# A two-layer hybrid diffusion block: Strassen products reordered, output sums regrouped, block-end splits deferred, modulation weights on GpSimd's queue

## The chip, the cores and the metric

The kernel runs on one core of a Trainium2 chip. The metric is device time in microseconds, the median over runs. Before the change it is 1779.36 us (two runs, 1778.30 and 1780.42).

## What is computed

Two layers over 512 latent and 256 context tokens of width 1024, all in float32. Cut to what matters here:

```python
for layer in range(2):
    mod_x = silu(c) @ ada_w[layer] + ada_b[layer]        # 6144 shifts, scales and gates; mod_c likewise from c_ctx
    hx = modulate(rmsnorm(x, norm1_g), sh1, sc1)         # and hc for the context
    mx, mc = hybrid_mixer(hx, hc, ...)                   # retention and gated linear attention
    x = x + g1 * (mx @ w_out)
    hx = modulate(rmsnorm(x, norm2_g), sh2, sc2)
    x = x + g2 * (square(relu(hx @ w_mlp1)) @ w_mlp2)    # 1024 -> 4096 -> 1024
    # in layer 0 the context goes the same way
return rmsnorm(x, final_g)
```

## The kernel before

Activations lie transposed, features on the 128 partitions and 768 tokens in the row. Each float32 operand is kept as a rounded part "hi" and a rest "lo", and each product is three matmuls: hi by hi, hi by lo, lo by hi (L525 to L527, L1409). Weights come in slabs of 128x1024 (512 KB) through SyncE's DMA queue into a pool of NRAW raw buffers; ScalarE casts hi (L246, L521) and VectorE subtracts for lo (L247, L522). Split slabs stand in a ring of NSPL = 5.

The order on every engine is that in which the program records its instructions. `run` (L467) goes through a list of items; before and after an item `advance` splits slabs up to AHEAD = 4 slabs ahead, as far as ring and raw buffers allow. Chains (ScalarE and VectorE steps that finish a product) are recorded a step at a time, at each tick.

The change acts on the MLP of layer 0. The 32 hidden tiles of 128 features are made in eight blocks of four. From the second block on, two tiles at a time (a "pair" j) are made by Strassen's scheme: seven products of 12 matmuls over 384 columns instead of eight (`strassen_items`, L1427). A `Pair` has four parts: part 0 holds a11 and a12, part 1 s2 and s3, part 2 s1 and a22, part 3 (in a ring of one) s4. The products are recorded as p1, p6, p7, p5, p2, p4, p3. ScalarE copies p1 out (L1450); VectorE adds the others up (L1444: u2, u3, c22, c21, c12). p2 is accumulated onto p1's PSUM bank, p4 onto p7's, p3 onto p5's, so each must follow the read of what the bank held. Of each output quarter, `hidden_chain` makes relu and square on ScalarE (hidh, L1422) and the rest on VectorE (hidl, L1425). After the two pairs of a block, `m2_part` multiplies the block's four hidden tiles by w_mlp2 (matmuls into `pm`) and VectorE adds the result to x (`residual`, L634). The first such item takes four banks and goes over hidden tiles 0 and 1 for all of them before it goes to tiles 2 and 3.

Between these items stand "ada" items. Each calls `ada_sums` (L389) once, which makes layer 1's modulation on VectorE: 64 steps, each with one 128x768 piece of ada_w, multiplied by two columns and added to two sums (L405 for the first of eight, then L407). After eight steps TensorE adds over the partitions (L415), ScalarE copies (L328), TensorE transposes (L333). The pieces come through SyncE's queue into the raw pool.

Of the kernel before, what the change touches and what calls it, by code (L numbers as in the profile page):

```python
# [16 lines left out]
P = 128  # L17
# [13 lines left out]
WCOL = 1024  # L31
NSLOT = 46
NSPL = 5
NRAW = 5
AHEAD = 4
# [3 lines left out]
class Item:  # L39


    def __init__(self, name, fn, slabs=(), deps=(), ahead=AHEAD):
        self.name, self.fn, self.slabs, self.deps, self.ahead = name, fn, list(slabs), list(deps), ahead


# [92 lines left out]
def build(ctx: ExitStack, tc, a):  # L138
# [29 lines left out]
    def chunks(t):  # L168
        return t.rearrange("p (c v) -> p c v", v=P)
# [219 lines left out]
    def ada_sums(l):  # L389
        acc = [work(f"adaacc_{l}_{v}") for v in range(2)]  # L390
        todo = [(u, kk) for u in range(6 * D // T) for kk in range(KK)]

        def load(i):
            u, kk = todo[i]
            w = wraw.tile([P, WCOL], F32, tag="raw", name=f"adaw_{l}_{u}_{kk}")
            nc.sync.dma_start(w[:, 0:T], a["ada_w"][l, kk * P : (kk + 1) * P, u * T : (u + 1) * T])
            return w[:, 0:T]

        nxt = load(0)
        for i, (u, kk) in enumerate(todo):  # L400
            w = nxt
            for v in range(2):
                c = cs[:, kk, v : v + 1]
                if kk == 0:
                    nc.vector.tensor_scalar(acc[v], w, c, None, op0=ALU.mult)  # L405
                else:
                    nc.vector.scalar_tensor_tensor(acc[v], w, c, acc[v], op0=ALU.mult, op1=ALU.add)  # L407
            if i + 1 < len(todo):
                nxt = load(i + 1)
            yield  # L410
            if kk == KK - 1:
                pt = psa.tile([P, 512], F32, tag="psa", name=f"ada_{l}_{u}")
# [54 lines left out]
    def run(plan):  # L467
# [9 lines left out]
        def load_next(must):  # L477

            nonlocal loaded
            if loaded == len(order):  # L480
                return False
            limit = NRAW - (2 if ada_queue else 1) - order[loaded].raws
            if order[loaded].raws and sum(x.held for x in order[:loaded]) > limit:
                assert not must
                return False
            order[loaded].load()
            loaded += 1
            return True
# [21 lines left out]
        for i, it in enumerate(plan):  # L510
            for s in it.slabs:
                need = max(need, order.index(s) + 1)
            advance(i, need + it.ahead)
            assert ready >= need, it.name
            it.fn()
            ch.tick()
            if it.slabs:
                advance(i + 1, need + AHEAD)
# [185 lines left out]
    seg = const.tile([P, T], U8, name="seg")  # L704
    maskb = const.tile([P, NCH, P], U8, name="maskb")
    lgam = const.tile([P, nrd], F32, name="lgam")
# [5 lines left out]
    def setup():  # L712
        nc.vector.memset(seg, 1.0)
        nc.vector.memset(chunks(seg)[:, :, 0:1], 0.0)
        for c in range(NCH):
            nc.vector.tensor_scalar(maskb[:, c], late["delta"], 0.0, None, op0=ALU.is_lt)

# [25 lines left out]
    def layer(l, norm):  # L743
# [29 lines left out]
        def tables(h):  # L773
# [4 lines left out]
            nc.scalar.activation(tmp, late["delta"], AF.Exp, scale=lgneg[:, gb : gb + 1])  # L778
            nc.vector.copy_predicated(d_, maskb[:, 0], tmp)
            nc.scalar.activation(rtab[:, 1], late["ramp"][:, 0], AF.Exp, scale=lgam[:, gf : gf + 1])  # L780
# [116 lines left out]
        def gla(h):  # L897
# [55 lines left out]
            def S():  # L953
# [10 lines left out]
                for (c0, c1), (pf, pb) in zip(CQ, pts):  # L964
                    n = (c1 - c0) * P
                    nc.scalar.copy(am[:, c0 * P : c1 * P], pf[:, 0:n])
                    nc.vector.copy_predicated(
                        am[:, c0 * P : c1 * P], maskb[:, c0:c1].rearrange("p c t -> p (c t)"), pb[:, 0:n]
                    )

# [456 lines left out]
        def strassen_items(j):  # L1427
# [24 lines left out]
            def p6():  # L1452
                product(pair, "s2", "t2", open_(2))
                out(2, "u2", st["p1"])

            def p7():
                product(pair, "s3", "t3", open_(3))
                out(3, "u3", st["u2"])

            def p5():  # L1460
                product(pair, "s1", "t1", open_(4))
                tail(out(4, "c22", st["u3"]), 1, H)

# [5 lines left out]

            def p4():  # L1470
                product(pair, "a22", "t4", p[3], False)
                tail(out(3, "c21", st["u2"]), 1, 0)

            def p3():
                product(pair, "s4", "b22", p[4], False)
                tail(out(4, "c12", st["u2"]), 0, H)

            for i, (fn, x) in enumerate(((p1, 0), (p6, 1), (p7, 1), (p5, 2), (p2, 0), (p4, 2), (p3, 3))):
                plan.append(Item(f"st{i}.{j}", fn, [pair.parts[x]]))
                if i % 2:  # L1480
                    plan.append(Item("ada", mlp_ada))
# [225 lines left out]
```

## Time and profile before

| | |
|---|---|
| median of two runs | 1779.36 us |
| profiled execution | 1778.82 us, span 1777.0 us |
| TensorE matmul busy | 1634.8 us (92%) |
| VectorE busy | 1076.0 us (61%) |
| ScalarE busy | 707.8 us (40%) |
| GpSimd busy | 152.8 us (9%) |
| DMA | 175.56 MB, 99 GB/s on average |

The page gives each engine's share of busy time in 40 slices of some 44 us; below them stands PEclk, the TensorE clock granted, in tenths of full speed. A list of waits names who waited for whom. A timeline row is: start, duration, engine, line, operation, output<-inputs, and in brackets the idle time just before it with its releaser. Matmuls of the same kind overlap, so their rate is read from the distance of their starts.

### The profile page before, as it was taken

The page shows a single profiled execution, that of the slowest core. Times are in us where ns is not written, and L with a number is a line of the kernel's source. Part 1 is how long each engine was busy: PE and PEld are TensorE (multiplying, and loading weights), DVE is VectorE, ACT ScalarE, POOL GpSimd, SP SyncE. Part 2 cuts the span into 40 slices and gives each one's busy share as a digit, 9 for nine tenths or more (in the row PEclk, how much of TensorE's full clock was granted, in tenths as well). Part 3 has the DMA queues.
Part 4 walks back from the last instruction along what each step waited for, and adds up shares of the span by engine and source line. Part 5 has one row for each costly group of instructions (what it writes and reads, how often), then busy time and mean ns, then how long its engine had stood idle before and what let it go on. Part 6 is the DMA issues. An engine that isn't in the chain of part 4 may idle for free.

```text
span 1777.0 us, 22807 instructions
## 1 busy us (share of the span) xinstructions
PE 1634.8 (92%) x9072; PEld 1404.2 (79%) x9072; DVE 1076.0 (61%) x1720; ACT 707.8 (40%) x1223; POOL 152.8 (9%) x159
## 2 busy tenths in 40 slices
PE   5899999999897978698879889999999899999998
PEld 3678888988796868587768777878888888888887
DVE  6575754656776767576667457658756744444445
ACT  5536335644623232332233244645355542222232
POOL 2200022100200000000000002000210210000000
PEclk9999999999998989899989999999999999999999
DMA  9334332221213333333334123122113323333311
GB/s 334 130 124 149 119 114 78 92 77 65 87 31 124 95 109 102 107 107 112 99 104 128 48 89 97 50 63 81 48 52 127 119 86 102 98 96 100 101 59 48
DMA packets 60777, 175.56 MB, mean 99 GB/s; under 512 B 6560, under 2 KB 18400, under 8 KB 60672
## 3 DMA queue, kind: packets, MB, share of 16 engines
q1 hardware_dynamic: 58400, 166.62, 29.2%
q0 software_dynamic: 2272, 7.50, 1.2%
q8 instruction: 71, 1.16, 0.3%
q14 instruction: 34, 0.28, 0.1%
HBM read 169.90 MB, written 4.19 MB: 98 GB/s over the span
## 4 chain that ended last, share of the span: by engine, by line
PE 64%; DVE 17%; ACT 8%; DMA 6%; issue 5%; SPq 0%; POOL 0%; DVEq 0%; ACTq 0%; POOLq 0%
PE pm L526 10%; PE pm L527 10%; PE pm L525 10%; DMA adaw<-in_ada_w 5%; DVE adaacc L407 4%; PE ps_g L527 2%; PE ps_g L525 2%; PE ps_g L526 2%; PE pro L1128 1%; DVE x L634 1%; PE ps_vr L526 1%; PE ps_vr L525 1%; PE ps_vr L527 1%; DVE lo_m L247 1%; PE ps_vg L525 1%
## 5 line engine op out<-in xcount | busy, mean ns | idle before, releaser
L526 PE MATMUL pm<-hidl,hi_m 128*128 128x512 f32 (+1 forms) x800 | 288.5, 361 | 29.6 <-DVE hidl L1425 25.8
L525 PE MATMUL pm<-hidh,hi_m 128*128 128x512 f32 (+1 forms) x800 | 288.5, 361 | 22.8 <-ACT hidh L1422 22.8
L527 PE MATMUL pm<-hidh,lo_m 128*128 128x512 f32 (+1 forms) x800 | 285.9, 357 | 0.0
L526 PEld LDWEIGHTS pm<-hidl,hi_m 128*128 128x128 f32 x800 | 157.6, 197 | 53.3 <-DVE hidl L1425 28.3
L525 PEld LDWEIGHTS pm<-hidh,hi_m 128*128 128x128 f32 x800 | 157.5, 197 | 48.5 <-ACT hidh L1422 24.4
L634 DVE SCALAR_TENSOR_TENSOR x<-pm,mod,x 128x512 f32<-128x512 f32 (+1 forms) x200 | 121.3, 641 | 112.3 <-PE pm L527 112.3
L527 PEld LDWEIGHTS pm<-hidh,lo_m 128*128 128x128 f32 x800 | 157.2, 197 | 20.5
L246 ACT CAST hi_m<-raw_m 128x1024 fp32r<-128x1024 f32 x100 | 104.1, 1041 | 93.2 <-PE pm L526 93.2
L407 DVE SCALAR_TENSOR_TENSOR adaacc<-adaw,cs,adaacc 128x768 f32<-128x768 f32 x112 | 108.8, 1013 | 50.3 <-DMA adaw<-in_ada_w 50.3
L526 PE MATMUL pm<-yl,hi_m 128*128 128x512 f32 (+1 forms) x352 | 128.0, 364 | 2.1 <-DVE yl L620 2.1
L525 PE MATMUL pm<-yh,hi_m 128*128 128x512 f32 (+1 forms) x352 | 128.3, 365 | 0.0
L527 PE MATMUL pm<-yh,lo_m 128*128 128x512 f32 (+1 forms) x352 | 127.7, 363 | 0.5 <-DVE lo_m L247 0.5
L247 DVE TENSOR_TENSOR lo_m<-raw_m,hi_m 128x1024 fp32r<-128x1024 f32 x98 | 120.1, 1226 | 11.5 <-ACT hi_m L246 8.5
L1323 DVE TENSOR_TENSOR hidl<-relu,hidh 128x512 fp32r<-128x512 f32 (+1 forms) x44 | 28.5, 649 | 160.9 <-POOL relu L1321 160.9
L1409 PE MATMUL pst<-yh,hi_m1s 128*128 128x384 f32 x224 | 76.9, 343 | 5.0 <-ACT p L1450 5.0
L526 PEld LDWEIGHTS pm<-yl,hi_m 128*128 128x128 f32 x352 | 67.4, 192 | 13.0 <-DVE yl L620 2.9
L247 DVE TENSOR_TENSOR lo_wi<-raw_wi,hi_wi 128x1024 fp32r<-128x1024 f32 x49 | 59.2, 1224 | 29.1 <-ACT hi_wi L246 29.1
L1409 PE MATMUL pst<-yl,hi_m1s 128*128 128x384 f32 x224 | 76.2, 340 | 0.0
L527 PEld LDWEIGHTS pm<-yh,lo_m 128*128 128x128 f32 x352 | 67.4, 191 | 10.9 <-DVE lo_m L247 1.0
L1409 PE MATMUL pst<-yh,lo_m1s 128*128 128x384 f32 x224 | 75.9, 339 | 0.0
L525 PEld LDWEIGHTS pm<-yh,hi_m 128*128 128x128 f32 x352 | 67.4, 191 | 10.1
L1319 ACT ACTIVATE relu<-pm 128x512 f32<-128x512 f32 (+1 forms) x44 | 23.6, 537 | 128.8 <-PE pm L527 128.8
(358 smaller groups left out, 3877.1 us busy)
## 6 DMA issues: line engine op xcount, KB each, us to landing
raw_m<-in_w_mlp SPq DMA_DIRECT2D x100, 512.0 KB, 3.4
raw_wi<-in_w_in SPq DMA_DIRECT2D x58, 512.0 KB, 3.5
adaw<-in_ada_w SPq DMA_DIRECT2D x64, 384.0 KB, 3.3
adaw<-in_ada_w SPq DMA_DIRECT2D x32, 512.0 KB, 4.7
raw_m1s<-in_w_mlp SPq DMA_DIRECT2D x28, 512.0 KB, 3.9
adaw<-in_ada_w SPq DMA_DIRECT2D x32, 256.0 KB, 6.3
raw_wo<-in_w_out SPq DMA_DIRECT2D x16, 512.0 KB, 3.5
x<-in_xT POOLq DMA_DIRECT2D x8, 384.0 KB, 3.6
```

Source lines behind the costliest of these rows:

```text
L246: nc.scalar.copy(self.hi, self.raw)
L247: self.engine.tensor_sub(self.lo, self.raw, f32(self.hi))
L407: nc.vector.scalar_tensor_tensor(acc[v], w, c, acc[v], op0=ALU.mult, op1=ALU.add)
L525: nc.tensor.matmul(out, wh, xh, start=first, stop=False)
L526: nc.tensor.matmul(out, wh, xl, start=False, stop=False)
L527: nc.tensor.matmul(out, wl, xh, start=False, stop=last)
L634: nc.vector.scalar_tensor_tensor(xs[kk][:, t0:t1], pt[:, 0 : t1 - t0], mod[l][:, v, gate + kk : gate + kk + 1], xs[kk][:, t0:t1], op0=ALU. ...
L1128: nc.tensor.matmul(dst, w, x, start=m == 0, stop=m == len(terms) - 1)
L1319: nc.scalar.activation(r, pt[:, 0 : t1 - t0], AF.Relu)
L1323: nc.vector.tensor_sub(a_.lo[:, t0:t1], r, f32(a_.hi[:, t0:t1]))
L1409: nc.tensor.matmul(pt[:, 0:H], wt[:, w], xt, start=first and k == 0 and i == 0, stop=k == KH - 1 and i == 2, skip_group_check=True,)
```

## The change

Strassen's products are recorded as p1, p6, p5, p7, p3, p4, p2. The sums become u2 = p1+p6, u4 = u2+p5, c22 = u4+p7, c12 = u4+p3, c21 = (p7 bank with p4 added)+u2, c11 = p1 bank with p2 added. p3 has a bank of its own. The last product of each block is marked quiet: no slab is split or loaded after it, and before the item that follows only as many as that item needs. The pieces of ada_w have two tiles of their own (two more slots of 128x768) and come through GpSimd's queue; there is one raw buffer less, and the rule that limits how many slabs are held is fitted to that. `ada_sums` gives up control twice more before L415. The mask of the attention scores is kept once and read through a repeating access pattern instead of six copies.

```diff
-NSLOT = 46
+NSLOT = 48
-NRAW = 5
+NRAW = 4
...
     def ada_sums(l):
         acc = [work(f"adaacc_{l}_{v}") for v in range(2)]
+        ws = [work(f"adaw_{l}_{i}") for i in range(2)]
...
-            w = wraw.tile([P, WCOL], F32, tag="raw", name=f"adaw_{l}_{u}_{kk}")
-            nc.sync.dma_start(w[:, 0:T], a["ada_w"][l, kk * P : (kk + 1) * P, u * T : (u + 1) * T])
-            return w[:, 0:T]
+            nc.gpsimd.dma_start(ws[i % 2], a["ada_w"][l, kk * P : (kk + 1) * P, u * T : (u + 1) * T])
+            return ws[i % 2]
...
             if kk == KK - 1:
+                yield
+                yield
...
-            limit = NRAW - (2 if ada_queue else 1) - order[loaded].raws
+            limit = NRAW - (2 if ada_queue else 0) - order[loaded].raws
...
-            advance(i, need + it.ahead)
+            advance(i, need + (0 if i and plan[i - 1].quiet else it.ahead))
...
-            if it.slabs:
+            if it.slabs and not it.quiet:
                 advance(i + 1, need + AHEAD)
...
-    maskb = const.tile([P, NCH, P], U8, name="maskb")
+    maskb = const.tile([P, P], U8, name="maskb")
...
-                    nc.vector.copy_predicated(
-                        am[:, c0 * P : c1 * P], maskb[:, c0:c1].rearrange("p c t -> p (c t)"), pb[:, 0:n]
-                    )
+                    nc.vector.copy_predicated(chunks(am)[:, c0:c1], rep(maskb, c1 - c0), chunks(pb[:, 0:n]))
...
+            def p5():
+                product(pair, "s1", "t1", open_(3))
+                out(3, "u4", st["u2"])
+
             def p7():
-                product(pair, "s3", "t3", open_(3))
-                out(3, "u3", st["u2"])
-
-            def p5():
-                product(pair, "s1", "t1", open_(4))
-                tail(out(4, "c22", st["u3"]), 1, H)
+                product(pair, "s3", "t3", open_(4))
+                tail(out(4, "c22", st["u4"]), 1, H)
+
+            def p3():
+                product(pair, "s4", "b22", open_(5))
+                tail(out(5, "c12", st["u4"]), 0, H)
+
+            def p4():
+                product(pair, "a22", "t4", p[4], False)
+                tail(out(4, "c21", st["u2"]), 1, 0)
...
-            for i, (fn, x) in enumerate(((p1, 0), (p6, 1), (p7, 1), (p5, 2), (p2, 0), (p4, 2), (p3, 3))):
+            steps = ((p1, 0), (p6, 1), (p5, 2), (p7, 1), (p3, 3), (p4, 2), (p2, 0))
+            for i, (fn, x) in enumerate(steps):
                 plan.append(Item(f"st{i}.{j}", fn, [pair.parts[x]]))
+                plan[-1].quiet = 2 * j % UT == 2 and i == 6
...
-    nc = _bacc.Bacc("TRN2", target_bir_lowering=False, num_devices=1, dynamic_dma_scratch_size=2048)
+    nc = _bacc.Bacc("TRN2", target_bir_lowering=False, num_devices=1, dynamic_dma_scratch_size=1024)
```

VectorE at a block's end (pairs 6 and 7, the fourth block), before. c_0_7 are the output sums of pair 7, hidl_14 and hidl_15 the rests of hidden tiles 2 and 3, lo_m slabs of w_mlp2, everything with m1s_8 belongs to the next pair's weights, x_0 is the first residual after the block's end:

```order
L1444 TENSOR_TENSOR c_0_7_6069<-pst_0_7_5994,u_0_7_5988 128x384
L407 SCALAR_TENSOR_TENSOR adaacc_0_4596<-adaw_3_6_6031,cs,adaacc_0_4596 128x768
L407 SCALAR_TENSOR_TENSOR adaacc_1_4597<-adaw_3_6_6031,cs,adaacc_1_4597 128x768
L1425 TENSOR_TENSOR hidl_15_6025<-c_0_7_6069,hidh_15_6024 128x384
L247 TENSOR_TENSOR lo_m_0_15_6080<-raw_m_0_15_5945,hi_m_0_15_6079 128x1024
L1444 TENSOR_TENSOR c_0_7_6099<-pst_0_7_6009,u_0_7_5988 128x384
L522 TENSOR_TENSOR lo_m1s_8_6105<-raw_m1s_8_0_5971,hi_m1s_8_6104 128x1024
L297 TENSOR_TENSOR s_m1s_8_6108<-raw_m1s_8_0_5971,raw_m1s_8_1_5973 128x512
L298 TENSOR_TENSOR raw_m1s_8_1_5973<-raw_m1s_8_1_5973 128x512
L1425 TENSOR_TENSOR hidl_14_6049<-c_0_7_6099,hidh_14_6048 128x384
L634 SCALAR_TENSOR_TENSOR x_0_3350<-pm_0_3_0_0_6111,mod_147,x_0_3350 128x512
```

The same place now (L406 is the old L405, L637 the old L634, L248 the old L247, L525 the old L522):

```order
L1444 TENSOR_TENSOR c_0_7_6020<-pst_0_7_5951,u_0_7_5934 128x384
L406 TENSOR_SCALAR adaacc_0_4591<-adaw_0_4593,cs 128x768
L406 TENSOR_SCALAR adaacc_1_4592<-adaw_0_4593,cs 128x768
L1425 TENSOR_TENSOR hidl_15_5967<-c_0_7_6020,hidh_15_5966 128x384
L1425 TENSOR_TENSOR hidl_14_6000<-c_0_7_6041,hidh_14_5999 128x384
L637 SCALAR_TENSOR_TENSOR x_0_3345<-pm_0_3_0_0_6046,mod_147,x_0_3345 128x512
L637 SCALAR_TENSOR_TENSOR x_0_3345<-pm_0_3_0_512_6047,mod_147,x_0_3345 128x256
L637 SCALAR_TENSOR_TENSOR x_1_3347<-pm_0_3_1_0_6048,mod_147,x_1_3347 128x512
L637 SCALAR_TENSOR_TENSOR x_1_3347<-pm_0_3_1_512_6049,mod_147,x_1_3347 128x256
L248 TENSOR_TENSOR lo_m_0_14_6103<-raw_m_0_14_5890,hi_m_0_14_6102 128x1024
L248 TENSOR_TENSOR lo_m_0_15_6107<-raw_m_0_15_5892,hi_m_0_15_6106 128x1024
L525 TENSOR_TENSOR lo_m1s_8_6115<-raw_m1s_8_0_5917,hi_m1s_8_6114 128x1024
```

Two lo_m and the first three steps of the next pair's split stand behind the first four residuals instead of among the last sums; hidl_14 is made from c_0_7_6041, which ScalarE takes from PSUM, and no longer from a VectorE sum.

ScalarE between the two pairs of a block (pair 6, then pair 7), before. L1467 is the copy of c11 with relu, hi_m1s_7 with 128x1024 is part 2 of pair 7, with 128x512 part 3, p_0_7 is p1 of pair 7:

```order
L1467 ACTIVATE c_0_6_5889<-pst_0_6_5795 128x384
L1422 ACTIVATE hidh_12_5891<-c_0_6_5889 128x384
L1423 ACTIVATE c_0_6_5889<-c_0_6_5889 128x384
L521 CAST hi_m1s_7_5896<-raw_m1s_7_1_5474 128x1024
L1421 ACTIVATE c_0_6_5912<-c_0_6_5912 128x384
...
L1423 ACTIVATE c_0_6_5934<-c_0_6_5934 128x384
L521 CAST hi_m1s_7_5939<-raw_m1s_7_0_5472 128x512
L246 CAST hi_m_0_12_5947<-raw_m_0_12_5709 128x1024
L1450 COPY p_0_7_5965<-pst_0_7_5951 128x384
```

The same place now (L1475 is c11's copy, L524 the old L521):

```order
L1475 ACTIVATE c_0_6_5877<-pst_0_6_5746 128x384
L1422 ACTIVATE hidh_12_5841<-c_0_6_5877 128x384
L1423 ACTIVATE c_0_6_5877<-c_0_6_5877 128x384
L524 CAST hi_m1s_7_5882<-raw_m1s_7_1_5509 128x1024
L524 CAST hi_m1s_7_5886<-raw_m1s_7_0_5507 128x512
L247 CAST hi_m_0_12_5894<-raw_m_0_12_5673 128x1024
L1450 COPY p_0_7_5911<-pst_0_7_5898 128x384
```

Part 2 of the second pair is split behind all sums of the first pair instead of two sums earlier, since its ring slot holds the first pair's part 0, which p2, now the last product, still reads.

## Rows read from the trace of the kernel before

**Rows 1.** Who waited for whom, TensorE, 515 to 1062 us: total us, times, longest.
```profile
PE pm L526 <- DVE hidl L1425: 25.8, 7, 4.1
PE pm L525 <- ACT hidh L1422: 22.8, 7, 4.7
PE ada L415 <- DVE adaacc L407: 19.5, 12, 6.0
PE pst L1409 <- DVE u L1444: 9.4, 6, 2.9
PE pst L1409 <- ACT p L1450: 5.0, 3, 2.3
PE adat L333 <- ACT adarow L328: 5.0, 4, 2.7
```

**Rows 2.** Windows: span, PE, PEld, DVE, ACT, POOL busy (count), PEclk, DMA share, GB/s.
```profile
515.00:1062.00 547.00, 459.56 (x2482) 412.09 (x2481) 357.89 (x524) 169.01 (x283) 0.00 (x0) 0.93 0.32 99
646.50:734.00 87.50, 70.57 (x374) 63.04 (x374) 59.94 (x85) 24.57 (x41) 0.00 (x0) 0.92 0.35 107
986.00:1058.00 72.00, 63.12 (x348) 58.16 (x348) 37.20 (x56) 24.50 (x41) 0.00 (x0) 0.95 0.18 59
```

**Rows 3.** Timeline, TensorE, the first m2 item behind the fourth block.
```profile
734.05 0.58 PE L525 MATMUL pm<-hidh,hi_m 128*128 128x512 f32 x1 [3.93 <-ACT hidh L1422]
738.60 0.80 PE L526 MATMUL pm<-hidl,hi_m 128*128 128x512 f32 x1 [3.97 <-DVE hidl L1425]
```

**Rows 4.** Timeline, VectorE, the same place.
```profile
728.87 1.95 DVE L407 SCALAR_TENSOR_TENSOR adaacc<-adaw,cs,adaacc 128x768 f32<-128x768 f32 x2 [0.89 <-DMA adaw<-in_ada_w]
730.73 0.55 DVE L1425 TENSOR_TENSOR hidl<-c,hidh 128x384 fp32r<-128x384 f32 x1
...
732.34 0.55 DVE L1444 TENSOR_TENSOR c<-pst,u 128x384 f32<-128x384 f32 x1
735.52 1.22 DVE L522 TENSOR_TENSOR lo_m1s<-raw_m1s,hi_m1s 128x1024 fp32r<-128x1024 f32 x1 [2.63 <-ACT hi_m1s L521]
...
737.99 0.55 DVE L1425 TENSOR_TENSOR hidl<-c,hidh 128x384 fp32r<-128x384 f32 x1
```

**Rows 5.** Timeline, ScalarE, the c11 chain of pair 7 and the cast behind it.
```profile
722.12 0.47 ACT L1467 ACTIVATE c<-pst 128x384 f32<-128x384 f32 x1
...
723.18 0.52 ACT L1423 ACTIVATE c<-c 128x384 f32<-128x384 f32 x1
723.61 1.04 ACT L246 CAST hi_m<-raw_m 128x1024 fp32r<-128x1024 f32 x1
```

**Rows 6.** Groups by line, 515 to 1062 us: busy us, mean ns, idle before.
```profile
L407 DVE SCALAR_TENSOR_TENSOR adaacc<-adaw,cs,adaacc 128x768 f32<-128x768 f32 x112 | 108.8, 1013 | 50.3 <-DMA adaw<-in_ada_w 50.3
L405 DVE TENSOR_SCALAR adaacc<-adaw,cs 128x768 f32<-128x768 f32 x16 | 9.1, 615 | 0.1
```

**Rows 7.** Page, DMA issues: KB each, median us from issue to landing.
```profile
raw_wi<-in_w_in SPq DMA_DIRECT2D x58, 512.0 KB, 3.5
...
x<-in_xT POOLq DMA_DIRECT2D x8, 384.0 KB, 3.6
```

**Rows 8.** Timeline, VectorE: residuals and steps late in a block.
```profile
768.12 1.94 DVE L407 SCALAR_TENSOR_TENSOR adaacc<-adaw,cs,adaacc 128x768 f32<-128x768 f32 x2
771.15 1.14 DVE L634 SCALAR_TENSOR_TENSOR x<-pm,mod,x 128x512 f32<-128x512 f32 x2 [0.49 <-PE pm L527]
776.39 1.94 DVE L407 SCALAR_TENSOR_TENSOR adaacc<-adaw,cs,adaacc 128x768 f32<-128x768 f32 x2
```

**Rows 9.** Timeline, TensorE: Strassen matmuls, starts at full and at half rate.
```profile
631.52 0.33 PE L1409 MATMUL pst<-yl,hi_m1s 128*128 128x384 f32 x1
631.70 0.33 PE L1409 MATMUL pst<-yh,lo_m1s 128*128 128x384 f32 x1
...
632.44 0.52 PE L1409 MATMUL pst<-yh,lo_m1s 128*128 128x384 f32 x1
632.76 0.52 PE L1409 MATMUL pst<-yh,hi_m1s 128*128 128x384 f32 x1
```

More of the change, by code (lines that the diff above doesn't have):

```diff
@@ L43, in __init__ @@
         self.name, self.fn, self.slabs, self.deps, self.ahead = name, fn, list(slabs), list(deps), ahead
+        self.quiet = False
 class Chains:
@@ L714, in setup @@
         nc.vector.memset(chunks(seg)[:, :, 0:1], 0.0)
-        for c in range(NCH):
-            nc.vector.tensor_scalar(maskb[:, c], late["delta"], 0.0, None, op0=ALU.is_lt)
+        nc.vector.tensor_scalar(maskb, late["delta"], 0.0, None, op0=ALU.is_lt)
         re = sp.tile([P, nrd], F32, name="re", bufs=1)
@@ L778, in tables @@
             nc.scalar.activation(tmp, late["delta"], AF.Exp, scale=lgneg[:, gb : gb + 1])
-            nc.vector.copy_predicated(d_, maskb[:, 0], tmp)
+            nc.vector.copy_predicated(d_, maskb, tmp)
             nc.scalar.activation(rtab[:, 1], late["ramp"][:, 0], AF.Exp, scale=lgam[:, gf : gf + 1])
@@ L1468, in p2 @@
                 tail(c, 0, 0, False)
[L1470 to L1476, printed above, removed]
-            for i, (fn, x) in enumerate(((p1, 0), (p6, 1), (p7, 1), (p5, 2), (p2, 0), (p4, 2), (p3, 3))):
+            steps = ((p1, 0), (p6, 1), (p5, 2), (p7, 1), (p3, 3), (p4, 2), (p2, 0))
+            for i, (fn, x) in enumerate(steps):
                 plan.append(Item(f"st{i}.{j}", fn, [pair.parts[x]]))
+                plan[-1].quiet = 2 * j % UT == 2 and i == 6
                 if i % 2:
```

## The prediction, made before the changed kernel ran

> **What bounds the kernel now.** I read the windows first, then TensorE's list of waits, then the timeline at one place. The windows show the one stretch that the change can shorten: from 515 to 1062 us, the MLP of layer 0, TensorE is busy 459.6 of 547 us at a granted clock of 0.93 [rows 2]. The list of waits names its idle time there: 25.8 + 22.8 = 48.6 us behind the hidden tiles (hidl, hidh), 19.5 behind adaacc, 9.4 behind the sum u, 5.0 behind the copy p, 5.0 behind adarow, in all 87.5 us [rows 1]. The first two come seven times, once per block.
>
> Idle time costs twice. Strassen's matmuls start 0.18 us apart at full rate and 0.32 us apart in other places [rows 9]: the two levels, 2.4 and 1.2 GHz. A mean of 0.93 over 547 us means 0.07 x 547 = 38 us lost by the clock, an estimate from that one row. In the last block, where fewer additions for the modulation are left, the clock is 0.95 with 37.2 us of VectorE work instead of 59.9, and still 72.0 us go by [rows 2]. I therefore charge 38 / 87.5 = 0.43 us of clock to each us of idle; the most that could go is 87.5 + 38 = 125 us.
>
> The timeline shows what the seven waits are. TensorE stands 3.93 us for hidh, works off the first half of the item, and stands 3.97 us for hidl [rows 3]. VectorE is the late one: between the last sums it waits 0.89 us for a piece of ada_w, adds 1.95 us of modulation, splits a slab, and only at 732.34 makes the last sum; then, for the next pair, it waits 2.63 us for ScalarE's cast and does three steps before the last hidl at 737.99 [rows 4]. So one engine, in order, has more in these 30 us than it can do.
>
> **The change, part by part.** The sum is against the profiled execution, 1778.8 us, which is 0.6 below the median.
>
> *Block end (48.6 us).* Two lo_m of 1.22 us and the wait of 0.89 us leave VectorE's queue ahead of the last sums: 3.3 of the 3.93 us. Behind the last sum the next pair's split goes: from 732.34 to 737.99 are 5.65 us, of which ScalarE's three steps need 723.18 + 0.52 - 722.12 = 1.6 [rows 5]; the 4.0 saved are the second wait. Since the last product is now p2, its result even skips VectorE's sum. What is deferred, two lo_m of 1.22 and the first split of the next pair, some 5 us, falls behind the first residuals, where the work on four banks covers it; without that cover it costs 5 us a block. I leave 0.6 a block, rounded up to 1: 7 us. Bounds: 0 and 48.6.
>
> *Modulation on GpSimd's queue (19.5 us).* VectorE waits 50.3 us for these pieces [rows 6], since they queue on SyncE behind slabs that wait for a buffer. Now a piece starts when the step before the last one is done. A transfer of the same size on that queue lands 3.6 us after issue [rows 7]; from the end of one step (768.12 + 1.94) to the start of the second next (776.39) are 6.3 us [rows 8], so 2.7 us are left. If VectorE is packed, a step and two residual pairs lie between, 1.94 + 2 x 1.14 = 4.2 us [rows 8], which is still enough. Two more calls stand between a group's last step and the sum over partitions. A call is two products apart, 2 x 12 x 0.18 = 4.3 us, or a tile of m2; two exceed the longest wait, 6.0 us. The 19.5 go; bounds 0 and 19.5. What is late next is the step itself, but nobody waits for it within a group. The 88 calls that are now needed are fewer than the 90 ada items, so nothing of it is left over for layer 1.
>
> First the row that speaks on this queue: of VectorE's operations on those pieces only L405 runs at a quick rate, 615 ns where L407 takes 1013 ns for the same 768 columns, 9.1 us in all [rows 6]. The Trainium skill (SBUF — State Buffer, "SBUF: two separate sides") says against this part of the change that GpSimd cannot write the descriptors of its transfers while VectorE runs an operation that takes both of its ports. By that rule the issues could be held for those 9.1 us at worst, spread over eight groups and within 2.7 us of slack each; the sum would be the same, and the rival on this queue gets a small chance.
>
> *The order of the products (9.4 + 5.0 us).* p's copy is now five products old when p2 needs its bank: 5.0 go, bounds 0 and 5.0. In the place of the wait for u comes one for c22. p4 is accumulated onto p7's bank, with one product (2.2 us) between where there were two (4.3). With VectorE as late as now, the six waits would each grow by 2.2 (13 us), and eight other pairs would wait up to 2.2 (17 us): 9.4 + 13 + 17 = 40 us at most, 0 at least if VectorE is on time. Relieved of its 50.3 us of waiting and of 5 us at each block's end, it is nearer to on time; I take 1 us a pair, 14 us.
>
> *A new wait: part 2 of the second pair.* Its ring slot holds part 0 of the first pair, which p2 reads last; p5, now third, needs it two products and two matmuls later, 4.7 us. In between stand c11's chain and the cast, 722.12 to 724.65, 2.5 us [rows 5], and lo, 1.22 us: 3.8 us. There is 0.9 us of slack if VectorE is on time. Behind the cast in ScalarE's queue wait two more casts and p's copy, for which VectorE's u2 waits. Bounds: 0, and 4 us a block as in the longest hidl wait [rows 1]. VectorE has a modulation step of 1.95 us just ahead; one such step late gives 1, two give 3; I take 2, so 14 us.
>
> *Edits together.* One raw buffer fewer: the slabs of w_in are loaded a slab later. I cost it at nothing, since SyncE runs several slabs ahead of the casts; without that cover a late load costs at most its 3.5 us [rows 7]. The mask through a repeating pattern, the setup's five fewer compares, the two tiles and the smaller descriptor buffer lie beside TensorE's work in the mixer; nothing.
>
> *Sum.* Idle left: 7 + 14 + 14 + 5 (adarow) = 40 of 87.5. Saved: 47.5, and 0.43 x 47.5 = 20.6 by the clock: 68 us. 1778.8 - 68 = **1711 us**.
>
> **The rivals.**
>
> *Nearly all waits go.* If VectorE is on time, c22 and part 2 cost nothing and 5 to 25 us are left. For it: VectorE is busy 59.9 of 87.5 us in a block [rows 2]. Against it: in a block of 70 us that is over 80%, in order, with waits for ScalarE between. At 5 us left: 82.5 x 1.43 = 118, so 1661 us; up to 1689. Chance 0.16.
>
> *VectorE stays late and the waits move inside the block.* The 5 us deferred lands in m2, where VectorE also has its residuals and most steps; it enters Strassen's products late, and c22 waits as long as u's longest, 2.9 us, in all 14 pairs (41 us), with part 2 at 2 (14), block ends at 1 (7) and adarow 5: 67 left. Saved 20.5 x 1.43 = 29: 1749 us; as a band 60 to 85 us left, 1740 to 1775. For it: six waits for u already. Chance 0.18.
>
> *The change does not do what it says.* The order shows that the splits moved, so this could only be a queue that makes up for it: the time stays, 1765 to 1800. Chance 0.07.
>
> *Slower: transfers on GpSimd's queue come late.* Place: each of 64 modulation steps, in VectorE's queue ahead of sums that TensorE waits for. It decides from a landing of 6.3 us on; to eat the 68 us and 36 more (2%) it needs 104 / 64 = 1.6 us a step, a landing of 7.9 us. At 8.5 us: 2.2 x 64 = 141 lost, 68 gained, 1852 us. For it: nothing in the trace has VectorE as busy beside that queue. Against it: 3.6 us for eight transfers of this size [rows 7]. Chance 0.05.
>
> **How the numbers follow.** The forecast has the remaining 0.54: 25 to 60 us of idle left, 62.5 and 27.5 saved, times 1.43: 1689 to 1740. 2% of 1779.4, about what a measurement of this kernel can tell from no change, is 36 us: 1744 and 1815. Faster: 0.54 + 0.16 + 0.04 of the late case = 0.74; slower 0.05; within 2% the other 0.21. The range takes in the forecast, most of the two cases beside it, and leaves out some 0.05 below and 0.15 above: 1668 to 1762.
>
> **What would show it.** In the changed profile: the waits for hidl L1425 and hidh L1422 together below 15 us; none of adaacc on a transfer worth naming, and none of TensorE at L416; new ones of pst on c L1444 and on lo_m1s, some 14 us each; the clock above 0.95 from 515 us to that stage's end, which comes some 68 us earlier; 64 issues by GpSimd landing in 3.6 to 5 us. It is wrong if VectorE idles on adaw, if pm waits for hidl as before, or if the stage ahead of 515 us grows.

## The result and the profile after

The changed kernel takes 1687.34 us (median of two runs, 1684.87 and 1689.80) against 1779.36: a ratio of 0.948, 95% interval 0.942 to 0.955, 92 us faster. The forecast was 1711 us, range 1668 to 1762. The profiled execution, by which the rows go, took 1689.80 us (span 1688.0), 89.0 us less than the profiled one before.

First the list of waits of the whole program: who waited for whom, total us, times, longest.

```profile
PE pst L1409 <- ACT hi_m1s L524: 4.0, 4, 1.0
...
PE pst L1409 <- DVE lo_m1s L525: 3.9, 6, 0.7
...
PE pst L1409 <- DVE c L1444: 3.7, 5, 0.9
...
PE ps_d L542 <- ACT hh_n L616: 3.0, 1, 3.0
PE adat L334 <- ACT adarow L329: 2.5, 4, 1.0
...
PE pm L529 <- DVE hidl L1425: 1.4, 3, 0.6
```

No hidh, no adaacc, no u, no p is among them any more [rows 1]; of hidl 1.4 us is left. What is new are the waits of the Strassen matmuls (pst) for the weights' split (hi_m1s and lo_m1s, part 2 of the second pair) and for c, where the prediction had put them, at 7.9 and 3.7 us instead of 14 each.

Then the window (span; PE, PEld, DVE, ACT, POOL busy; PEclk; DMA share; GB/s) of the MLP stage, from the first Strassen matmul to the first matmul of layer 1.

```profile
524.49:1001.97 477.48, 462.62 (x2636) 420.46 (x2635) 371.75 (x549) 181.09 (x301) 40.70 (x72) 0.99 0.37 118
```

The same stretch before lasted 575.0 us (519.09 to 1094.10). It is 97.5 us shorter, and the clock is 0.99 where it was 0.93 [rows 2]. TensorE's idle time in it, summed over the bracketed times of the timeline, fell from 87.4 to 14.6 us. The rest is slow matmuls: I counted those whose distance to the next start, less idle time, is over one and a half times what it is at full rate. Before they took 36.3 us too much (210 of them), after 14.2 (102). So 72.8 us are idle time, 22.1 slow matmuls (an estimate: with the matmuls right before a wait counted as well it is some 26) and 2.6 neither.

A block's end on TensorE, then on VectorE (start, duration, what; in brackets the idle time before it and its releaser):

```profile
765.93 0.50 PE L529 MATMUL pm<-hidl,hi_m 128*128 128x512 f32 x1 [0.40 <-DVE hidl L1425]
```
```profile
763.89 0.55 DVE L1425 TENSOR_TENSOR hidl<-c,hidh 128x384 fp32r<-128x384 f32 x1
765.32 0.56 DVE L1425 TENSOR_TENSOR hidl<-c,hidh 128x384 fp32r<-128x384 f32 x1 [0.87 <-ACT c L1423]
767.42 1.19 DVE L637 SCALAR_TENSOR_TENSOR x<-pm,mod,x 128x512 f32<-128x512 f32 x2 [1.54 <-PE pm L530]
```

Where TensorE stood 3.93 and 3.97 us [rows 3] it stands 0.40. VectorE goes from the last hidl straight to the residuals and is early for them: it waits 1.54 us for TensorE. No split stands between [rows 4].

The modulation's pieces, from the page and from the view of the issuing line (duration of one issue min/median/max in ns):

```profile
L408 DVE SCALAR_TENSOR_TENSOR adaacc<-adaw,cs,adaacc 128x768 f32<-128x768 f32 x112 | 108.2, 1009 | 0.0
...
adaw<-in_ada_w POOLq DMA_DIRECT2D x64, 384.0 KB, 3.5
```
```profile
L397 POOL DMA_DIRECT2D adaw<-in_ada_w x64: 536/536/579, 507.7 to 933.2; - x64
```

VectorE's 50.3 us of waiting for them [rows 6] are gone; they land 3.5 us after issue in the median, 5.3 at the longest.

### The profile page after: what moved, and what is told of

It reads as the page before. It is cut to its first block, busy times and chain, and to the rows that moved or that the text cites. A ratio compares the mean times of both kernels' runs of the same rounds, so it can differ in the third digit from the quotient of the medians.

```text
span 1688.0 us, 22837 instructions
## 1 busy us (share of the span) xinstructions
PE 1613.8 (96%) x9072; PEld 1390.4 (82%) x9072; DVE 1070.6 (63%) x1715; ACT 708.1 (42%) x1223; POOL 187.3 (11%) x223
## 3 DMA queue, kind: packets, MB, share of 16 engines
q1 hardware_dynamic: 49184, 141.45, 25.4%
## 5 line engine op out<-in xcount | busy, mean ns | idle before, releaser
L529 PE MATMUL pm<-hidl,hi_m 128*128 128x512 f32 (+1 forms) x800 | 279.8, 350 | 5.3 <-DVE hidl L1323 3.8
L528 PE MATMUL pm<-hidh,hi_m 128*128 128x512 f32 (+1 forms) x800 | 280.1, 350 | 0.0
L530 PE MATMUL pm<-hidh,lo_m 128*128 128x512 f32 (+1 forms) x800 | 278.6, 348 | 0.0
L529 PEld LDWEIGHTS pm<-hidl,hi_m 128*128 128x128 f32 x800 | 152.1, 190 | 26.1 <-DVE hidl L1323 4.3
L637 DVE SCALAR_TENSOR_TENSOR x<-pm,mod,x 128x512 f32<-128x512 f32 (+1 forms) x200 | 120.6, 640 | 80.0 <-PE pm L530 79.9
L528 PEld LDWEIGHTS pm<-hidh,hi_m 128*128 128x128 f32 x800 | 152.1, 190 | 21.6 <-issue 1.9
L530 PEld LDWEIGHTS pm<-hidh,lo_m 128*128 128x128 f32 x800 | 151.9, 190 | 19.5
L247 ACT CAST hi_m<-raw_m 128x1024 fp32r<-128x1024 f32 x100 | 103.6, 1043 | 93.2 <-PE pm L529 93.2
L248 DVE TENSOR_TENSOR lo_m<-raw_m,hi_m 128x1024 fp32r<-128x1024 f32 x98 | 118.8, 1224 | 7.8 <-ACT hi_m L247 4.7
L408 DVE SCALAR_TENSOR_TENSOR adaacc<-adaw,cs,adaacc 128x768 f32<-128x768 f32 x112 | 108.2, 1009 | 0.0
L397 POOL DMA_DIRECT2D adaw<-in_ada_w x64 | 34.5, 538 | 413.4 <-DVE adaacc L408 248.3
L248 DVE TENSOR_TENSOR lo_wi<-raw_wi,hi_wi 128x1024 fp32r<-128x1024 f32 x49 | 59.5, 1225 | 32.6 <-ACT hi_wi L247 32.5
L1321 POOL TENSOR_TENSOR relu<-relu 128x512 f32<-128x512 f32 (+1 forms) x44 | 42.4, 965 | 338.1 <-ACT hidh L1320 337.7
L1319 ACT ACTIVATE relu<-pm 128x512 f32<-128x512 f32 (+1 forms) x44 | 23.6, 536 | 128.4 <-PE pm L530 128.3
```

Source lines behind the costliest of these rows:

```text
L247: nc.scalar.copy(self.hi, self.raw)
L248: self.engine.tensor_sub(self.lo, self.raw, f32(self.hi))
L397: nc.gpsimd.dma_start(ws[i % 2], a["ada_w"][l, kk * P : (kk + 1) * P, u * T : (u + 1) * T])
L528: nc.tensor.matmul(out, wh, xh, start=first, stop=False)
L529: nc.tensor.matmul(out, wh, xl, start=False, stop=False)
L530: nc.tensor.matmul(out, wl, xh, start=False, stop=last)
```

## The experiments

All are compared with the kernel before on the same chip (1778.4 to 1779.4 us). Unless said otherwise each is the changed kernel with one edit; "the order" is that of the products together with the regrouped sums.

| kernel | pieces of ada_w | two more calls | quiet | order | us | ratio, 95% | stage | idle |
|---|---|---|---|---|---|---|---|---|
| before | SyncE, raw pool | no | no | old | 1779.4 | 1 | 575.0 | 87.4 |
| e12_mask_only | SyncE, raw pool | no | no | old | 1778.7 | 0.9983–1.0004 | 571.8 | 88.4 |
| e11_queue_yields | GpSimd, own tiles | yes | no | old | 1751.8 | 0.9825–0.9857 | 540.4 | 61.2 |
| e5_ada_only | GpSimd, own tiles | no | no | old | 1748.7 | 0.9817–0.9850 | 534.8 | 59.5 |
| e6_order_only | SyncE, raw pool | no | yes | new | 1748.2 | 0.9810–0.9844 | 541.6 | 63.0 |
| e2_ada_sync | SyncE, raw pool | yes | yes | new | 1724.2 | 0.9680–0.9709 | 518.0 | 42.2 |
| e3_old_order | GpSimd, own tiles | yes | yes | old | 1721.5 | 0.9653–0.9693 | 515.3 | 40.7 |
| e8_own_tiles_sync | SyncE, own tiles | yes | yes | new | 1710.7 | 0.9595–0.9631 | 497.4 | 27.0 |
| e4_no_yields | GpSimd, own tiles | no | yes | new | 1709.4 | 0.9594–0.9626 | 495.7 | 29.6 |
| e9_mixed_order | GpSimd, own tiles | yes | yes | old/new | 1700.3 | 0.9538–0.9572 | 488.9 | 23.6 |
| e10_second_pair | GpSimd, own tiles | yes | yes | second pair between | 1694.5 | 0.9504–0.9536 | 482.5 | 22.9 |
| e14_p2_last | GpSimd, own tiles | yes | yes | old, p2 last | 1693.0 | 0.9499–0.9527 | 484.2 | 24.4 |
| the change | GpSimd, own tiles | yes | yes | new | 1687.3 | 0.942–0.955 | 477.5 | 14.6 |
| e1_no_quiet | GpSimd, own tiles | yes | no | new | 1685.5 | 0.9462–0.9497 | 475.0 | 14.9 |

Stage and idle are those of the profiled run, taken as above. By and large the time follows the idle time; neighbours change places (e14 has 0.8 us more of it than e9 and takes 7 us less). The interval of the change, from two runs, is wide and takes in e10 and e14; that of e1, on the same level from four runs, lies below theirs.

**The change without the quiet mark.**
```diff
-                plan[-1].quiet = 2 * j % UT == 2 and i == 6
```


> The change without the quiet mark: at each block's end slabs are split again right behind the last product. Theory A (the block-end waits are work that stands ahead of the last hidl in VectorE's queue, so what counts is where the splits are recorded): two lo_m, the next pair's first split and ScalarE's casts stand ahead of hidl again; hidl waits of 3 to 4 us come back at each of seven blocks, 21 to 28 us, with the clock 30 to 40 us in all: 1717 to 1727 us. Theory B (VectorE was late because of its 50 us of waiting for the pieces of ada_w, and that is cured by the queue alone): VectorE is early enough to do the splits in between; under 5 us lost, 1687 to 1692 us.

It took 1685.45 us: within the new order the mark is worth nothing. That is close to theory B's time, but not for B's reason; the premise of A fails. VectorE at a block's end:

```profile
762.01 0.56 DVE L1425 TENSOR_TENSOR hidl<-c,hidh 128x384 fp32r<-128x384 f32 x1 [0.88 <-ACT c L1423]
762.95 2.36 DVE L248 TENSOR_TENSOR lo_m<-raw_m,hi_m 128x1024 fp32r<-128x1024 f32 x2 [0.37 <-ACT hi_m L247]
```

The two lo_m stand behind the last hidl without the mark too. With p2 last, part 0 of the second pair keeps its ring slot until p2 has read it, so by the program's rule they can't be split ahead of the block's last sums. The mark moves only the first four residuals ahead of the splits; hidl's wait is 2.6 us without it, 1.4 with it.

**The pieces back on SyncE's queue and in the raw pool.**
```diff
-            nc.gpsimd.dma_start(ws[i % 2], a["ada_w"][...])
-            return ws[i % 2]
+            w = wraw.tile([P, WCOL], F32, tag="raw", ...)
+            nc.sync.dma_start(w[:, 0:T], a["ada_w"][...])
+            return w[:, 0:T]
```
(with NRAW, NSLOT and the limit as before)

> The change with the pieces of ada_w back in the raw pool and on SyncE's queue (5 raw buffers, 46 slots, the old limit); order, quiet and the two more calls stay. Theory A: VectorE waits for pieces again, some 50 us, but behind the block's end nothing stands ahead of hidl; half of the waiting reaches TensorE through c and lo_m1s: 15 to 25 us idle, 1708 to 1723 us. Theory B: most of the gain goes, 1745 us or more. It also tells whether the 5.4 us that the stretch ahead of the Strassen products lost (first Strassen matmul at 524.5 instead of 519.1 us) come from the raw buffer taken away: then it starts near 519 us again, else near 524.

1724.21 us: 37 slower than the change. TensorE's waits, then VectorE's, 505 us to the stage's end:

```profile
PE pst L1409 <- ACT hi_m1s L524: 14.4, 5, 3.3
PE pst L1409 <- DVE c L1444: 7.3, 6, 3.5
PE adat L334 <- ACT adarow L329: 6.2, 2, 5.8
PE pm L528 <- ACT hidh L1422: 5.8, 4, 2.6
```
```profile
DVE adaacc L408 <- DMA adaw<-in_ada_w: 43.0, 21, 3.4
```

VectorE's 43 us of waiting for pieces come back, and with them waits of TensorE, foremost at these four places; the one for adaacc itself is 0.3 us. A late VectorE shows up at whatever TensorE wants next. The time is 1 us above theory A's range; the idle time, 42.2 us, is far above A's 15 to 25.

**The old order of products and sums.**
```diff
-            steps = ((p1, 0), (p6, 1), (p5, 2), (p7, 1), (p3, 3), (p4, 2), (p2, 0))
+            steps = ((p1, 0), (p6, 1), (p7, 1), (p5, 2), (p2, 0), (p4, 2), (p3, 3))
```
(with u3, c22, c21, c12 as before; queue, calls and quiet mark kept)

> The change with Strassen's products and sums in the old order (p1, p6, p7, p5, p2, p4, p3), quiet behind p3; queue, tiles and calls stay. Theory A: the last result needs VectorE's sum (0.55 us) and then ScalarE's three steps and hidl, 2.7 us, against 4.1 us of cover in the first m2 item, so the block ends stay mostly free; the waits for part 2 (7.9 us in the changed kernel) go and waits for u and p come, under 10 us: 1680 to 1700 us. Theory C (the order is what freed the block's end): waits for hidh and hidl of 3 us a block, 30 us with the clock, 1717 us.

1721.53 us, 34 slower than the change. TensorE's list of waits, whole program:

```profile
PE pm L528 <- ACT hidh L1422: 19.4, 6, 3.3
PE pst L1409 <- DVE u L1444: 12.3, 9, 2.9
...
PE pm L529 <- DVE hidl L1425: 3.4, 7, 0.7
```

This is theory C. hidh's half of the block-end wait and u's are what the order takes away; hidl's is down to 3.4 us here already. VectorE, then TensorE, at the end of the third block in this kernel:

```profile
634.90 1.23 DVE L248 TENSOR_TENSOR lo_m<-raw_m,hi_m 128x1024 fp32r<-128x1024 f32 x1 [0.38 <-ACT hi_m L247]
636.04 0.55 DVE L1444 TENSOR_TENSOR c<-pst,u 128x384 f32<-128x384 f32 x1
```
```profile
637.75 0.80 PE L528 MATMUL pm<-hidh,hi_m 128*128 128x512 f32 x1 [3.30 <-ACT hidh L1422]
```

Two splits of w_mlp2 still stand among the last sums in spite of the quiet mark, this one and a like one at 630.57, each with a wait of 0.38 us for its cast: 2 x (1.23 + 0.38) = 3.2 us, about TensorE's 3.30. In the change none stands there (VectorE's rows in the section above).

**Without the two more calls.**
```diff
             if kk == KK - 1:
-                yield
-                yield
```


> The change without the two more calls between a group's last step and the sum over partitions. Theory A: with the pieces on time, the last step is done a call (4 us) before L418 needs it, so TensorE waits under 1 us in each of eight groups; and VectorE's steps are packed into 72 calls instead of 88, which costs up to 2 us a block at c and lo_m1s: 1688 to 1700 us. Theory D (the calls are what took the 19.5 us of waiting): waits for adaacc come back at 10 to 20 us, with the clock 1702 to 1716 us.

1709.42 us, 22 slower. This is theory D. TensorE's list of waits has it stand at the sum over the partitions:

```profile
PE ada L416 <- DVE adaacc L408: 17.6, 6, 6.2
```

Against e5 and e11 below this shows a dependence: in the old order without the quiet mark the same wait is 3.0 us without the calls, none with them, and the two kernels take 1748.7 and 1751.8 us. With the pieces on SyncE's queue but the new order the calls are worth 24 us (e6 below to e2, adaacc's wait 36.7 to 0.3). So they pay only where the block-end waits, behind which the step was finished, are gone.

**The queue and its tiles alone; the order alone.** e5 has of the change only the pieces' tiles and queue (and the mask); e6 only the order and the quiet mark (and the mask).

> Of the change only the pieces of ada_w on GpSimd's queue in tiles of their own (with the buffers and the limit that go with them, and the single mask): old order of products and sums, no quiet, no two more calls. Leaving the queue out of the change cost 37 us, the order 34, the two calls 22, quiet nothing. Theory A2 (three separate waits, each removed by its own part, so the parts add): 37 us off, 1735 to 1750 us; VectorE's wait for pieces gone, block-end waits for hidl still near 4 us each, adaacc waits near 20 us. Theory B2 (VectorE's lateness is one quantity that any part relieves, so the first part takes most): 60 us or more off, below 1720 us.

> Of the change only the new order with the regrouped sums and quiet (and the single mask): pieces on SyncE's queue and in the raw pool, no two more calls. Theory A2: 34 us off, 1738 to 1752 us, waits for hidl L1425 under 5 us, adaacc waits near 20 us, part-2 waits of 10 to 20 us. Theory B2: below 1720 us.

1748.69 and 1748.18 us: 30 us each, where taking either out of the change costs 37 and 34. Both times are A2's and B2 is out; but A2's adaacc waits near 20 us are not there (3.0 and 36.7), and the two parts alone make 60 of the 92 us, so the parts don't add. e6's waits, TensorE and VectorE:

```profile
PE ada L416 <- DVE adaacc L408: 36.7, 9, 9.5
...
PE pm L526 <- ACT hidh L1420: 3.5, 3, 1.9
PE pm L527 <- DVE hidl L1423: 3.2, 5, 0.7
```
```profile
DVE adaacc L408 <- DMA adaw<-in_ada_w: 41.4, 22, 3.4
```

The order alone takes the block-end wait from 48.6 [rows 1] to 6.7 us, but adaacc's grows from 19.5 to 36.7: part of the gain is handed on to a wait that the block ends had covered.

**The own tiles kept, the transfers issued by SyncE.**
```diff
-            nc.gpsimd.dma_start(ws[i % 2], ...)
+            nc.sync.dma_start(ws[i % 2], ...)
```


> The change with the two own tiles kept, but their transfers issued on SyncE's queue. Theory Q (the gain of 37 us comes from the queue: a piece on SyncE stands behind slabs that wait for a raw buffer): VectorE waits for pieces 30 us or more, 1712 to 1728 us. Theory T (it comes from the tiles: a piece no longer takes a raw buffer from the slabs): within 5 us of the change, 1682 to 1692 us.

1710.67 us, 23 slower than the change, 14 faster than e2: of the 37 us the queue is worth about two thirds, the tiles and what goes with them one third. From the lists, TensorE's wait at the block end and VectorE's for pieces:

```profile
PE pm L528 <- ACT hidh L1422: 9.0, 4, 2.7
```
```profile
DVE adaacc L408 <- DMA adaw<-in_ada_w: 17.0, 7, 3.1
```

VectorE's wait is below Q's 30 us and the time just below Q's range; T is out. In the median the pieces land in 3.3 us there, no slower than on GpSimd's queue. But the seven that VectorE waits for were issued 6.8 to 12.0 us after their tile had come free, right behind two slabs of the next weights, and landed only in 5.5 to 6.1 us. One of them, SyncE and VectorE:

```profile
548.18 1.46 SPq L289 DMA_DIRECT2D raw_m1s<-in_w_mlp  x2
549.69 0.43 SPq L397 DMA_DIRECT2D adaw<-in_ada_w  x1
```
```profile
540.96 1.94 DVE L408 SCALAR_TENSOR_TENSOR adaacc<-adaw,cs,adaacc 128x768 f32<-128x768 f32 x2
...
555.84 1.02 DVE L408 SCALAR_TENSOR_TENSOR adaacc<-adaw,cs,adaacc 128x768 f32<-128x768 f32 x1 [3.10 <-DMA adaw<-in_ada_w]
```

Its tile was free at 542.90, when the step of 540.96 ended; SyncE reached the piece at 549.69, behind the slabs.

**First pair of a block in the old order; second pair with p5 back behind p7.** In e9 the first pair has the old order and sums, the second the new. In e10 the first has the new, the second p1, p6, p7, p5, p4, p3, p2 with the old sums.

> The change with the first pair of each block in the old order and with the old sums, the second in the new. The changed kernel's waits for part 2 (3.9 on lo_m1s, 4.0 on its cast) exist because the first pair's p2, now last, holds the ring slot that part 2 of the second pair takes. Theory A: with p2 fifth in the first pair the slot is free two products earlier, 7.9 us of waits go and with the clock 10 to 12 us: 1673 to 1680 us. Rival: in the old order p waits for its copy and p4 for u, and slabs are split between the sums again, so as much comes back: 1685 to 1700 us.

> The change, but the second pair of each block runs p1, p6, p7, p5, p4, p3, p2 with the old sums (u3, c22, c21, c12): part 2 of the new slab is wanted one product (2.2 us) later, p2 stays last. Theory P (the part-2 stalls, 7.9 us in the changed kernel with 0.6 to 1.0 us each, only want 2.2 us more room): they go, with 0.43 us of clock per us, and the price is a wait of p4 for u3 or c22 on p7's bank, with p5 alone between, as in the first pair (3.7 us over five there): 1687 - (7.9 - 3.7) x 1.4 = 1681, 1676 to 1685. Rival R (the early p5 is what lets VectorE get ahead of the pair's sums; any other order moves the wait to p4, as it did with p2 in the middle, 15.1 us over five stalls): c or u waits of 10 to 16 us, 1690 to 1702.

1700.30 and 1694.49 us, 13 and 7 slower. In both the part-2 waits are gone, and another has come (TensorE's list, of e9, then of e10):

```profile
PE pst L1409 <- DVE c L1444: 15.1, 5, 4.0
```
```profile
PE pst L1409 <- DVE u L1444: 16.2, 6, 3.6
```

In e9 theory A fails and the time is at the edge of the rival's; but the price is not at p or u: all five waits for c are those of the second pair's p4 for c22, with splits ahead of it on VectorE (as at 612.90 and 614.51). In e10 this is the rival, R: giving part 2 one product more room puts p4 one product behind the sum u3 that its bank must have given up. The 7.9 us are the cheaper of the two.

**The queue and the calls in the old order, without the quiet mark.** This is e3 without the mark.
```diff
-                plan[-1].quiet = 2 * j % UT == 2 and i == 6
```


> The kernel before with the pieces of ada_w on GpSimd's queue in own tiles and the two more calls, but the old order of products and sums and no held-back split. With the held-back split the same kernel took 1721.5 us. Theory K (the split is worth something where p2 is not last, since the slab's splits then stand ahead of the last sums): hidl and hidh waits come back to some 35 to 40 us from 22.8 with it, 1733 to 1742. Rival L (held back or not, the order of products sets where the splits stand): 1719 to 1725, hidl and hidh together 20 to 25.

1751.82 us, 30 slower than e3; theory K has the sign and too small a size. TensorE's list:

```profile
PE pm L529 <- DVE hidl L1425: 25.4, 7, 4.0
PE pm L528 <- ACT hidh L1422: 17.9, 6, 3.3
```

So the mark, worth nothing in the new order, is worth 30 us in the old one (with queue and calls), where p2 in the middle frees a ring slot and the splits would stand ahead of the last sums: it takes hidl's wait from 25.4 to 3.4 and leaves hidh's (17.9 here, 19.4 in e3).

**The old sums, but p2 last.** This is e3 with one line changed:
```diff
-            steps = ((p1, 0), (p6, 1), (p7, 1), (p5, 2), (p2, 0), (p4, 2), (p3, 3))
+            steps = ((p1, 0), (p6, 1), (p7, 1), (p5, 2), (p4, 2), (p3, 3), (p2, 0))
```


> The changed kernel with the old sums (u3, c22, c21, c12) and the order p1, p6, p7, p5, p4, p3, p2 in every pair: of the reordering only p2's place at the end is kept, p5 goes back behind p7 and u4 goes. With p2 in the middle as well the same kernel took 1721.5 us. Theory S (p2 at the end is what clears the block end, the regrouping only keeps p4 from waiting for its sum): hidh and hidl together under 4 us instead of 22.8, no part-2 waits, u waits as in the second pairs of the run before (16.2 us over six, so some 30 over fourteen); idle 38 us, against 14.6 in the change: 1687 + 23 x 1.3 = 1717, 1707 to 1721. Rival W (the regrouping does most of it: VectorE's sums are late in the old grouping wherever p2 stands, and come late for the block end too): hidh 15 to 20 as with the old order, u on top, 1722 to 1740.

1692.97 us, 28.6 faster than e3 and 5.6 slower than the change. The waits of the whole program, and the stage's window:

```profile
PE pst L1409 <- DVE u L1444: 23.0, 11, 2.6
...
PE pm L529 <- DVE hidl L1425: 0.6, 1, 0.6
```
```profile
522.24:1006.48 484.24, 459.86 (x2636) 420.91 (x2635) 372.46 (x549) 181.10 (x301) 40.60 (x72) 0.99 0.37 116
```

Theory S holds: p2's place clears the block end, hidh is gone; the regrouping and p5's early place only turn 23.0 us of u into 3.7 of c and 7.9 of part 2. It came out below S's range, first because 24.4 us of idle time were left and not 38 (u 23.0 and not some 30), then because these waits of at most 2.6 us left the clock at 0.99: the slow matmuls cost 12.0 us, in the change 14.2.

**The mask and the descriptor buffer alone.**

> The kernel before with one 128-column mask read through a repeating pattern and the 1024-byte descriptor buffer, nothing else. All changed kernels so far have the first Strassen matmul 2 to 7 us later than before (519.1 us). Theory M (one of these two is the cause): 1781 to 1786, first Strassen matmul at 521 to 526. Rival N (it is the other parts, or the start-up of the single run): 1777 to 1780, first Strassen matmul at 518 to 520.

1778.68 us against 1778.48 on the same chip. By time it is N: the two are worth nothing. By the marker it looks like M: the first Strassen matmul is at 523.46, 4.4 us later than before, and the stage 3.2 us shorter. A marker in one profiled run is not a cost.

## Why the prediction was right, and where its sizes were off

**What bounds the kernel** was right: VectorE late at one place per block, in this stage. Everything gained was gained there.

**Block end.** Predicted 7 us left, measured 1.4. The steps were right, the two lo_m ahead of the last sums (3.3 us then; 3.2 in e3, where they alone stand there) and the next pair's split behind them. What I did not see is which edit moves which: p2's place takes out the lo_m, since part 0's ring slot is then held until the end (e3 to e14: hidh's 19.4 us gone), and the next pair's split goes by either p2's place or the mark (e11 to e3: hidl from 25.4 to 3.4; e1: 2.6 without the mark). That p2's result skips VectorE's sum was not tried apart from its place, so how much of the 28.6 us from e3 to e14 is the ring slot and how much the skipped sum is not shown; e3's rows (3.2 of 3.30 us) speak for the slot.

**Modulation on GpSimd's queue.** Right: no wait of VectorE for a piece, landing 3.5 us where 6.3 were allowed. Issues took 536 to 579 ns. The rule of the Trainium skill (SBUF — State Buffer, "SBUF: two separate sides") that the prediction weighed was not put to the test: none of the 64 issues runs at the same time as one of the quick steps (L406). Beside the operations that they do meet, such as L1444, L637 and L408, no issue was 50 ns longer than the shortest. The two calls did what was said, 22 us by e4; the price of leaving them out is not 19.5 us but depends on what else waits.

**c22.** Predicted 14 us, measured 3.7: five of fourteen pairs, 0.9 at most. I took a wait of 1 us in every pair for a late VectorE; it came in five, in one of them with only 0.16. [Rows 1]'s u waits were a poor guide, since VectorE was then behind by pieces and splits.

**Part 2 of the second pair.** Predicted 14, measured 7.9. I said that late modulation steps on VectorE, just ahead, would make the difference, 2 us a block. Half of it came by another road. Here is the place in the third block: TensorE, then ScalarE, then VectorE.

```profile
611.79 0.45 PE L1409 MATMUL pst<-yh,hi_m1s 128*128 128x384 f32 x1 [1.03 <-ACT hi_m1s L524]
...
613.05 0.45 PE L1409 MATMUL pst<-yh,lo_m1s 128*128 128x384 f32 x1 [0.64 <-DVE lo_m1s L525]
```
```profile
609.22 0.47 ACT L1475 ACTIVATE c<-pst 128x384 f32<-128x384 f32 x1
...
610.71 1.55 ACT L524 CAST hi_m1s<-raw_m1s 128x1024 fp32r<-128x1024 f32 x2
```
```profile
599.04 1.94 DVE L408 SCALAR_TENSOR_TENSOR adaacc<-adaw,cs,adaacc 128x768 f32<-128x768 f32 x2
600.90 0.55 DVE L1444 TENSOR_TENSOR u<-pst,u 128x384 f32<-128x384 f32 x1
601.55 0.56 DVE L1444 TENSOR_TENSOR c<-pst,u 128x384 f32<-128x384 f32 x1
...
606.61 0.56 DVE L1425 TENSOR_TENSOR hidl<-c,hidh 128x384 fp32r<-128x384 f32 x1 [1.71 <-ACT c L1423]
607.09 0.55 DVE L1444 TENSOR_TENSOR c<-pst,u 128x384 f32<-128x384 f32 x1
```

From c11's copy (609.22) to the first matmul are 2.57 us, my 2.5. But p2 was through at 606.59, and the copy starts 2.6 us after that: it stands on ScalarE behind the chain of c21, c21's sum (607.09) on VectorE behind a hidl, and that hidl 1.71 us behind ScalarE's chain of c12, which stands in the same way behind that of c22. From c22's sum (601.55) to c11's copy this queue takes 7.67 us. The slack of 0.9 us left it out.

c22's sum is late in its turn: p7 was through at 599.19, but VectorE came to u4 only after a modulation step (599.04). So the late step is on the path after all, further ahead than I had put it. In the second block VectorE makes u2 2.5 us before p7 is through (here 0.6), the step behind it is a short one (1.14 us), and c22 is on time, at 533.02; the queue takes as long (7.66 us), the copy is 1.5 us late, and only lo_m1s is waited for, 0.65 us. I read from this: about 0.65 us in six blocks (lo_m1s, 3.9 in all) belong to the queue that I left out, about 1.0 in four (hi_m1s, 4.0) to VectorE's lateness ahead of c22. How much of that lateness is the step and how much the splits ahead of u2 is not shown.

**The clock.** I charged 0.43 us per us of idle time; the slow matmuls fell by 22.1 for 72.8, so 0.30. A wait has no fixed price. Four windows of 10 us: in e10 and in e11 from the last 0.9 us of a single wait on (3.63 and 4.05 us long), in e11 one with hidl's 3.75 us just behind hidh's 3.30, in e14 from the last 0.9 us of a wait of 2.31 us on:

```profile
618.00:628.00 10.00, 9.11 (x42) 8.90 (x43) 5.95 (x10) 5.53 (x11) 1.08 (x2) 0.83 0.48 152
```
```profile
721.80:731.80 10.00, 9.08 (x34) 7.64 (x35) 4.81 (x8) 0.62 (x1) 0.00 (x0) 0.66 0.01 2
562.00:572.00 10.00, 5.65 (x16) 4.42 (x17) 4.22 (x6) 1.98 (x3) 0.00 (x0) 0.51 0.19 58
```
```profile
600.60:610.60 10.00, 9.07 (x52) 9.07 (x53) 7.58 (x12) 5.93 (x12) 1.61 (x3) 1.00 0.26 80
```

0.83 and 0.66 behind the single ones, 0.51 (near the lower level, 1.2 of 2.4 GHz) around the two, 1.00 behind the short one; yet another wait of 2.31 us in e14, at 670.77, left 0.83. The length of a wait alone does not tell what it costs. Over the whole stage the clock is 0.99 in e14 and in e10 too.

**Edits costed at nothing.** The mask and the descriptor buffer cost nothing (e12). The raw buffer fewer, or the two own tiles that came with it, do cost something: layer 1 begins with a wait that the kernel before has not.

```profile
1025.20 0.39 PE L542 MATMUL ps_d<-hh_n,hi_wi 128*128 128x256 f32 x1 [3.00 <-ACT hh_n L616]
```

From layer 1's first matmul to the end it takes 682.4 to 682.9 us in the four kernels with five raw buffers (before, e2, e6, e12) and 685.3 to 687.3 in the ten with four, e8 with its SyncE queue among them. That is 3.1 us in the change, within the 3.5 that I gave a late load at most; four raw buffers and own tiles always came together, so which of them it is stays open.

**The sum again.** 68 us were predicted to be saved. 25.4 us more idle time went than I had left (40 to 14.6, which is 1.4 + 3.7 + 7.9 and 1.5 for adarow), at 1.43 that is 36; the lower clock charge on 72.8 us takes 9.2 off; 2.5 us of the stage's gain are in neither; ahead of the stage 5.4 us were lost, behind it 3.1. 68 + 36 − 9.2 + 2.5 − 8.5 = 89, the difference of the profiled runs. The 5.4 us ahead of the stage I have not explained: they are 2 to 7 in every kernel I ran, e12 among them; with five raw buffers the stage starts at 522.63 in e2 and at 521.14 in e6, so the buffer alone is not the cause. The prediction had named a longer stretch ahead of the stage as a sign of being wrong, and this sign came.

What came, then, has the size of what I had priced as the rival "nearly all waits go" (5 to 25 us of idle left, 1661 to 1689 us, chance 0.16), though not its reason: c22 and part 2 are not nothing but 11.6 of the 14.6 us left. The forecast's own band, 1689 to 1740 us, is missed by 2 us. And the number is in part luck: at my price the idle time alone would have made 104 us, 1675; a smaller clock charge and 8.5 us lost outside the stage, neither foreseen, brought it to 1687. The step that was off is the remainder of 7 + 14 + 14 us, and in it c22 above all: I carried VectorE's lateness of the old kernel over to one from which 50 us of waiting had been taken.

No variant beats the change beyond the intervals; e1, without the mark, is level with it.

## What to carry to other kernels

An in-order engine that is late at one place pays at whatever is wanted next, so the worth of an edit depends on the others: the quiet mark is worth 30 us or nothing, the two calls 22 or nothing, and the order alone moved 17 us into another wait. Look at what a product's place holds (a ring slot, a bank) and which work that lets in ahead of the late engine's sums, before regrouping arithmetic: p2's place was worth 28.6 us, the regrouped sums with p5's early place 5.6, which the two runs of the change hardly tell from nothing. Small pieces with a deadline do not belong in a queue behind large loads that wait for buffers; the same transfers, as quick to land in the median, were 23 us better on a queue of their own.

## What was not expected of the hardware

Transfers of 384 KB issued by GpSimd beside a VectorE that is 78% busy (371.75 of 477.48 us) landed in 3.5 us in the median, no later than the eight of that size before [rows 7]. On SyncE's queue, right behind two slabs of 512 KB, seven of them took 5.5 to 6.1 us. And the same wait of TensorE, 2.31 us in e14, left the clock at 1.00 in one place and at 0.83 in another.
